# A split matmul on one core: twenty Strassen pairs in place of eighteen, evacuations shared out per visit, and one transfer per pair of row blocks

## The chip, the core and the metric

The kernel runs on one core of a Trainium2 chip. The metric is the device time of the whole program in microseconds, the median of several runs. The engines named below are TensorE (PE, with its weight loads PEld), VectorE (DVE), ScalarE (ACT), GpSimd (POOL) and SyncE (SP).

## What is computed

```python
batch, m, k, n = 16, 512, 1024, 768
grad_weight = np.einsum('bmk,bmn->kn', input, grad_output)     # float32
```

With the batch folded into the rows this is one product: the transpose of X (8192 x 1024) times G (8192 x 768), summed over 8192 rows. The result is 1024 x 768 in float32.

## The kernel before, in words

**Slices and pairs.** The 8192 rows are 64 slices of 128 rows; a slice is the depth of one matmul. Slices come in 32 pairs (u = 0 to 31), each with a tile xp (128 partitions x 2 x 1024, bfloat16) and gp (128 x 2 x 768). GpSimd issues the transfers (lines 99 to 102), one for each slice's part of gp and of xp, and they convert float32 to bfloat16 on the way. Only slice 0 and the x part of slice 1 come as float32 through SyncE and ScalarE (lines 72 to 77) and are cast by VectorE and ScalarE (`round_by`, line 191). The pool holds 14 pairs (`PAIRS_HELD`).

**Products.** The result is cut in four: A (upper half of the rows, left half of the columns), B (upper right), C (lower left) and D (lower right), each 512 x 384. A slice alone ("s" in `LOADS`) adds one product to each of A, B, C and D: 4 products. A pair treated as a 2 x 2 block ("P") takes Strassen's way with 7 products in place of 8: two of them go straight into A and D, and five into the side sums m, n, o, p and q (`macc`). Each product is 4 matmuls of 128 x 384, one for each of 4 PSUM banks (q = 0 to 3), so that a slice costs 16 matmuls, and a pair 28 in place of 32. `LOADS` says which pairs are taken in which way: 18 are "P".

**Sums.** A "P" pair needs sums of its operands before its products, six VectorE instructions (lines 114 to 143): g1 (`ge` 0 and 1), g2 (`ge` 2), g3 (in place in `gp`), x1 (`xe` 0 and 1), x2 (`xe` 2) and x3 (in place in `xp`). What a product needs of them: m needs x2 and g2; n and q need x1; o and p need g3; A and D need x3 and g1 (`operands`, line 212).

**Shares.** Near the end the five side sums are added to and taken from the result, 24 VectorE instructions: `top1` to `top3` for the upper half, `low1` to `low3` for the lower half, each for 4 values of q. Eight of them (`top3`, `low3`) are 384 wide, the others 768.

**Visits, banks and the order.** PSUM has eight banks, in two slots of four. A visit in `ORDER` continues one product stream in an open slot: "A17" multiplies all items of stream A up to but not including its 17th (counted over all items for A, B, C and D; the streams m to q count pairs alone). With "!" it then closes: each bank is evacuated into SBUF (`acc` or `macc`). Before, the banks 0 and 1 are evacuated by VectorE, which adds the bank to the sum (line 284; below such an instruction is called V), and the banks 2 and 3 by ScalarE, which copies (line 280). So that ScalarE need only copy, the sum so far is copied into the bank when the visit opens (line 256), and the matmuls go on adding to it. A visit of one item does its four matmuls and then evacuates; a visit of several finishes bank after bank.

**What sets the order.** PE, VectorE and ScalarE run in exactly the order in which the program issues (`manual_schedule`, line 70). `ORDER` is written out: the figure ahead of the letter says how many of the waiting sums and shares (the list `filler`) VectorE does before the visit; the four figures behind "!" say how many it does before each bank's evacuation. An instruction of VectorE that waits holds all behind it. GpSimd's transfers are ordered by the tile framework, which has eight of them in flight.

**The tail.** The last visit, D46 before, does its last bank in two parts of 256 and 128 columns (line 312). Finished parts of A, B, C and D are stored by SyncE (lines 288 and 325).

A step from `ORDER`, as an example: `3m10!1,0,0,0` is three sums, then stream m up to pair 10, one sum, and the evacuation of its four banks.

Of the kernel before, what the change touches and what calls it, by code (L numbers as in the profile page):

```python
# [7 lines left out]

P = 128

LOADS = "sssPssssPsPsPPPPPPPPPPPPPPPsssss"


ORDER = (
    "A1 C1!0,0,0,0 D1 D2!0,0,0,0 A2 B1 B2 B3!0,0,0,0 A3 C4!0,0,0,0 A4 A5 B4 B5 B6!0,0,0,0 A6 "
    "C6!0,0,0,0 D6 6A7 D8!0,0,0,0 A8 o1!0,0,0,0 A9 B8!0,0,0,0 A10 C9 C10!0,0,0,0 A11 "
    "q1!0,0,0,0 A12 D12 A13 D13 A14!0,0,0,0 D14!0,0,0,0 n1 C14!0,0,0,0 B13 B14 6n2!0,0,0,0 "
    "B15 p1 p2!0,0,0,0 B16!0,0,0,0 m1 m2 A17!0,0,1,1 D18 4m3!0,0,0,0 D19 D20 B18!0,0,0,0 "
    "C18!0,0,1,1 A21 D21 4A22!0,0,0,0 D22 o4!2,0,1,1 q4 2D23!3,0,0,0 q5 n5 3n6!0,0,0,0 q6 p5 "
    "p6!6,0,0,0 q7 o7!1,0,0,2 m7 3q8!1,0,0,0 m8 A25 A26!5,0,0,0 m9 p9!1,0,0,2 D27 "  # L20
    "3m10!1,0,0,0 D28 n10!3,0,0,2 D29 A29!2,0,1,1 o11 2o12!2,0,0,0 D30 q12 4D31!1,0,0,0 q13 "
    "p12 p13!5,0,0,0 q14 m14!2,1,0,1 n14!2,0,0,2 q15 o15 4q16!0,0,0,0 o16 D34!2,0,1,1 "
    "A34!1,1,0,3 o17 n17 3o18!0,0,0,0 n18!0,0,0,0 A35 m18!0,0,0,0 A39 q18!0,0,0,0 p18!0,0,0,0 "
    "A41 A43 C22 C24 C26 A46!13,0,0,0 B23 B24 B28!6,0,0,0 C28!5,0,0,0 D46!0,0,0,0 "
).split()

WARMUP = [512] * 10 + [128] * 2
PAIRS_HELD = 14
SUMS_HELD = 9

CARRIED = (2, 3)
COPIED = CARRIED or (1, 3)


@with_exitstack
def kernel(
# [6 lines left out]
    nc = tc.nc  # L43
# [4 lines left out]
    _, _, N = grad_output.shape  # L48
    S = B * M // P
    KH = K // 2  # L50
    NH = N // 2
    Q = KH // P

    X = input.rearrange("b m k -> (b m) k")
    G = grad_output.rearrange("b m n -> (b m) n")
# [17 lines left out]
    gf = pairs.tile([P, N], f32, name="gf", tag="gp")  # L73
# [18 lines left out]
    xg = []  # L92
    for u, kind in enumerate(LOADS):
        pool = pairs if u else head
        xp = pool.tile([P, 2, K], bf16, name="xp", tag="xp")
        gp = pool.tile([P, 2, N], bf16, name="gp", tag="gp")
        for h in range(2):
            s = 2 * u + h
            if s > 0:
                nc.gpsimd.dma_start(out=gp[:, h, :], in_=G[s * P : (s + 1) * P, :])  # L100
            if s > 1:
                nc.gpsimd.dma_start(out=xp[:, h, :], in_=X[s * P : (s + 1) * P, :])  # L102
            if kind == "s":
                items.append(("s", xp[:, h, :], gp[:, h, :]))
        if kind == "P":
            items.append(("P", xp, gp))
        xg.append((xp, gp))
# [68 lines left out]
    filler = []  # L176
    for i, item in enumerate(items):
        if item[0] == "P":
            filler += [(f, i) for f in (sum_g1, sum_g2, sum_g3, sum_x1, sum_x2, sum_x3)]
    if filler:  # L180
        filler += [(f, q) for q in range(Q) for f in (top1, top2, top3)]
        filler += [(f, q) for q in range(Q) for f in (low1, low2, low3)]
    filler.reverse()

    def fill(n):
        for _ in range(n):
            f, i = filler.pop()
            f(i)


    def round_by(engine, dst, src, c0, c1):
        copy = nc.vector.tensor_copy if engine == "DVE" else nc.scalar.copy
        copy(out=dst[:, c0:c1], in_=src[:, c0:c1])  # L193

    x0, x1, g0 = items[0][1], items[1][1], items[0][2]
# [34 lines left out]
    def sum_of(p, q):  # L230
        if p in SLOT:
            return macc[:, SLOT[p], q, :]
        row = q if p in "AB" else Q + q
        return acc[:, row, 0:NH] if p in "AC" else acc[:, row, NH:N]

    done = {p: 0 for p in streams}
    fresh = {p: True for p in streams}
    slots = [0, 1]
    used = set()

    def visit(p, upto, close, ahead, last):
        items_now = streams[p][done[p] : upto]
        done[p] = upto
        opening = p not in opened
        if opening:

            tail = p in "ABCD" and streams[p][upto - len(items_now)] > LAST_PAIR - 2
            slot = slots.pop(0)
            banks = []
            for q in range(Q):  # L250
                name = f"bank{slot * Q + q}"
                bank = psum.tile([P, 512], f32, name=name)[:, 0:NH]
                carried = q in CARRIED and not fresh[p] and not tail
                if carried:
                    assert name in used
                    nc.scalar.copy(out=bank, in_=sum_of(p, q))  # L256
                used.add(name)
                banks.append((bank, carried))
            opened[p] = (slot, banks)
        slot, banks = opened[p]  # L260
        final = upto == len(streams[p])

        def mm(q, j):
            stat, mov = operands(p, items_now[j], q)
            bank, carried = banks[q]
            nc.tensor.matmul(  # L266
                bank,
                stat,
                mov,
                start=opening and j == 0 and not carried,  # L270
                stop=close and j == len(items_now) - 1,
                skip_group_check=carried,
            )

        def shut(q):
            fill(ahead[q])
            bank, carried = banks[q]
            dst = sum_of(p, q)
            if carried or (fresh[p] and q in COPIED):
                nc.scalar.copy(out=dst, in_=bank)  # L280
            elif fresh[p]:
                nc.vector.tensor_copy(out=dst, in_=bank)  # L282
            else:
                nc.vector.tensor_add(out=dst, in0=bank, in1=dst)  # L284
            if final and p in "ABCD":
                row = q if p in "AB" else Q + q
                c0 = 0 if p in "AC" else NH
                nc.sync.dma_start(out=OUT[:, row, c0 : c0 + NH], in_=dst)

        if len(items_now) == 1:  # L290
            for q in range(Q):
                mm(q, 0)
            if close:
                for q in range(Q):
                    shut(q)
        else:
            for q in range(Q):
                if last and q == Q - 1 and opening:
                    break
                for j in range(len(items_now)):  # L300
                    mm(q, j)
                if close:
                    shut(q)
            else:
                q = None
            if q is not None:

                fill(ahead[q])
                dst = sum_of(p, q)
                row = q if p in "AB" else Q + q  # L310
                b0 = 0 if p in "AC" else NH
                for c0, c1, name in ((0, 256, None), (256, NH, f"bank{slots[0] * Q}")):
                    bank = banks[q][0] if name is None else psum.tile([P, 512], f32, name=name)
                    for j in range(len(items_now)):
                        stat, mov = operands(p, items_now[j], q)
                        nc.tensor.matmul(  # L316
                            bank[:, 0 : c1 - c0],
                            stat,
                            mov[:, c0:c1],
                            start=j == 0,  # L320
                            stop=j == len(items_now) - 1,
                        )
                    d = dst[:, c0:c1]
                    nc.vector.tensor_add(out=d, in0=bank[:, 0 : c1 - c0], in1=d)  # L324
                    nc.sync.dma_start(out=OUT[:, row, b0 + c0 : b0 + c1], in_=d)
        if close:
            fresh[p] = False
            del opened[p]
            slots.append(slot)

    for n, step in enumerate(ORDER):
        step, _, ahead = step.partition("!")
        at = next(c for c in step if c.isalpha())
        before, upto = step.split(at)
        if n == 2:
            round_by("DVE", g0, gf, NH, N)
            round_by("DVE", x1, xf[1], 4 * P, 6 * P)
            round_by("ACT", x1, xf[1], 6 * P, 8 * P)
            round_by("DVE", x1, xf[1], 0, 2 * P)
            round_by("ACT", x1, xf[1], 2 * P, 4 * P)  # L340
        fill(int(before or 0))
        ahead = [int(a) for a in ahead.split(",")] if ahead else None
        visit(at, int(upto), ahead is not None, ahead, n == len(ORDER) - 1)
    assert not filler and not opened


# [28 lines left out]
```

## Time and profile before

| | |
|---|---|
| time, median of 3 | 169.47 us (169.4 to 169.53) |
| span of the profile | 168.0 us |
| granted TensorE clock | 1.000 |
| PE, DVE, ACT, POOL busy | 161.3, 124.1, 73.3, 66.6 us |
| one matmul of 128 x 384, by the records | 327 ns (it overlaps the next) |
| V: evacuating add of a bank, 128 x 384 | 553 ns |
| ScalarE copy out of a bank, into a bank | 483 ns, 496 ns |
| a share of 768, of 384 columns | 954 ns, 558 ns |
| x and g transfers of GpSimd | 62 and 63, 8.5 us from issue to landing |
| DMA, GB/s written in the middle | 206 to 211 |

How to read it: the records of matmuls overlap, so their duration is not their spacing. An instruction of VectorE or ScalarE can also start before the one ahead of it has ended, which is why spacings are read from the starts in the timeline. A wait of an engine that isn't the bottleneck costs nothing. A slot, below, is the time of one matmul, and slots are counted from the first matmul that is not a warm-up: the matmul numbers follow from `ORDER`.

### The profile page before, as it was taken

The page shows a single profiled execution, that of the slowest core. Times are in us where ns is not written, and L with a number is a line of the kernel's source. Part 1 is how long each engine was busy: PE and PEld are TensorE (multiplying, and loading weights), DVE is VectorE, ACT ScalarE, POOL GpSimd, SP SyncE. Part 2 cuts the span into 40 slices and gives each one's busy share as a digit, 9 for nine tenths or more (in the row PEclk, how much of TensorE's full clock was granted, in tenths as well). Part 3 has the DMA queues.
Part 4 walks back from the last instruction along what each step waited for, and adds up shares of the span by engine and source line. Part 5 has one row for each costly group of instructions (what it writes and reads, how often), then busy time and mean ns, then how long its engine had stood idle before and what let it go on. Part 6 is the DMA issues. An engine that isn't in the chain of part 4 may idle for free.

```text
span 168.0 us, 2737 instructions
## 1 busy us (share of the span) xinstructions
PE 161.3 (96%) x976; PEld 95.3 (57%) x976; DVE 124.1 (74%) x248; ACT 73.3 (44%) x172; POOL 66.6 (40%) x129
## 2 busy tenths in 40 slices
PE   8799989999999999999999899999999999989991
PEld 2365545656666566555566466655666666556561
DVE  0642755307667686999999988999996179999992
ACT  3536608435456473654554643365655451000000
POOL 7444444454355444455444554445526430000000
PEclk9999999999999999999999999999999999999999
DMA  5999999999999999999999999999999999331546
GB/s 180 287 209 209 206 210 209 208 206 211 209 208 209 208 209 208 209 207 208 209 208 209 207 207 209 211 207 208 208 208 210 208 208 208 65 134 53 187 151 223
DMA packets 21036, 33.39 MB, mean 199 GB/s; under 512 B 2336, under 2 KB 12832, under 8 KB 21024
## 3 DMA queue, kind: packets, MB, share of 16 engines
q0 software_dynamic: 18000, 28.65, 93.2%
q1 hardware_dynamic: 2736, 3.54, 6.0%
q10 hardware_dynamic: 288, 1.05, 1.6%
q8 instruction: 7, 0.11, 0.3%
q14 instruction: 5, 0.04, 0.1%
HBM read 58.72 MB, written 3.15 MB: 368 GB/s over the span
## 4 chain that ended last, share of the span: by engine, by line
PE 74%; DMA 12%; DVE 9%; POOL 2%; issue 1%; DVEq 0%; POOLq 0%
PE bank L266 73%; DMA xp<-in_input_dram 12%; DVE acc L152 5%; DVE acc L163 1%; POOL gp L100 1%; DVE macc L284 1%; PE bank L316 1%; POOL xp L102 1%; DVE xp L143 0%; DVE xe L134 0%; DVE acc L284 0%; DVE gp L129 0%; DVE acc L324 0%; DVE ge L124 0%; DVE xe L138 0%
## 5 line engine op out<-in xcount | busy, mean ns | idle before, releaser
L266 PE MATMUL bank<-gp,xp 128*128 128x384 bf16 x582 | 102.2, 327 | 1.9 <-DVE gp L193 0.9
L266 PEld LDWEIGHTS <-xp 128*128 128x128 bf16 x724 | 70.6, 98 | 51.1 <-issue 2.7
L102 POOL DMA_DIRECT2D xp<-in_input_dram x62 | 33.0, 532 | 42.9 <-DMA xp<-in_input_dram 30.4
L100 POOL DMA_DIRECT2D gp<-in_grad_output_dram x63 | 33.7, 536 | 27.5 <-DMA gp<-in_grad_output_dram 16.0
L284 DVE TENSOR_TENSOR acc<-bank,acc 128x384 f32<-128x384 f32 x53 | 27.0, 553 | 15.2 <-PE bank L266 15.0
L280 ACT COPY acc<-bank 128x384 f32<-128x384 f32 x46 | 20.5, 483 | 31.6 <-PE bank L266 31.6
L280 ACT COPY macc<-bank 128x384 f32<-128x384 f32 x46 | 20.5, 483 | 31.0 <-PE bank L266 31.0
L266 PE MATMUL bank<-ge,xp 128*128 128x384 bf16 x142 | 28.7, 326 | 0.7 <-DVE xp L143 0.6
L266 PEld LDWEIGHTS <-xe 128*128 128x128 bf16 x216 | 21.1, 98 | 14.3 <-issue 0.4
L266 PE MATMUL bank<-gp,xe 128*128 128x384 bf16 x144 | 26.3, 326 | 0.0
L284 DVE TENSOR_TENSOR macc<-bank,macc 128x384 f32<-128x384 f32 x36 | 18.6, 554 | 7.7 <-PE bank L266 7.6
L256 ACT COPY bank<-acc 128x384 f32<-128x384 f32 x38 | 17.2, 495 | 0.0
L256 ACT COPY bank<-macc 128x384 f32<-128x384 f32 x36 | 16.3, 496 | 0.0
L152 DVE TENSOR_TENSOR acc<-acc,macc 128x768 f32<-128x768 f32 x16 | 15.3, 954 | 0.3
L266 PE MATMUL bank<-ge,xe 128*128 128x384 bf16 x72 | 13.0, 326 | 0.0
L143 DVE TENSOR_TENSOR xp<-xp 128x1024 bf16<-128x1024 bf16 x18 | 12.4, 688 | 0.0
L134 DVE TENSOR_TENSOR xe<-xp 128x1024 bf16<-128x1024 bf16 x18 | 12.4, 687 | 0.0
L120 DVE TENSOR_TENSOR ge<-gp 128x768 bf16<-128x768 bf16 x18 | 10.0, 553 | 1.0 <-DMA gp<-in_grad_output_dram 0.8
L129 DVE TENSOR_TENSOR gp<-gp 128x768 bf16<-128x768 bf16 x18 | 9.9, 553 | 0.0
L282 DVE COPY acc<-bank 128x384 f32<-128x384 f32 x8 | 4.1, 553 | 7.7 <-PE bank L266 7.7
L282 DVE COPY macc<-bank 128x384 f32<-128x384 f32 x10 | 5.1, 553 | 3.8 <-PE bank L266 3.8
L138 DVE TENSOR_TENSOR xe<-xp 128x512 bf16<-128x512 bf16 x18 | 7.6, 421 | 0.0
(18 smaller groups left out, 27.5 us busy)
## 6 DMA issues: line engine op xcount, KB each, us to landing
xp<-in_input_dram POOLq DMA_DIRECT2D x62, 256.0 KB, 8.5
gp<-in_grad_output_dram POOLq DMA_DIRECT2D x63, 192.0 KB, 8.5
out_dram<-acc SPq DMA_DIRECT2D x15, 192.0 KB, 2.0
xf<-in_input_dram ACTq DMA_DIRECT2D x2, 512.0 KB, 5.0
gf<-in_grad_output_dram SPq DMA_DIRECT2D x2, 192.0 KB, 4.5
out_dram<-acc SPq DMA_DIRECT2D x1, 128.0 KB, 2.1
out_dram<-acc SPq DMA_DIRECT2D x1, 64.0 KB, 1.8
```

What stands on the lines that cost most here:

```text
L100: nc.gpsimd.dma_start(out=gp[:, h, :], in_=G[s * P : (s + 1) * P, :])
L102: nc.gpsimd.dma_start(out=xp[:, h, :], in_=X[s * P : (s + 1) * P, :])
L120: nc.vector.tensor_add(out=ge[:, 0:2, :], in0=g[:, :, 0, :], in1=g[:, :, 1, :])
L129: nc.vector.tensor_sub(out=g[:, 1:3, :], in0=g[:, 1:3, :], in1=g[:, 3::-3, :])
L134: nc.vector.tensor_add(out=xe[:, 0:2, :].rearrange("p a k -> p (a k)"), in0=xp[:, 0, :], in1=xp[:, 1, :])
L143: nc.vector.tensor_sub(out=x[:, 1:3, :], in0=x[:, 1:3, :], in1=x[:, 0::3, :])
L152: nc.vector.tensor_add(out=dst, in0=dst, in1=macc[:, slots, q, :])
L256: nc.scalar.copy(out=bank, in_=sum_of(p, q))
L266: nc.tensor.matmul(bank, stat, mov, start=opening and j == 0 and not carried, stop=close and j == len(items_now) - 1, skip_group_check=car ...
L280: nc.scalar.copy(out=dst, in_=bank)
L282: nc.vector.tensor_copy(out=dst, in_=bank)
L284: nc.vector.tensor_add(out=dst, in0=bank, in1=dst)
```

## The change

Twenty pairs are taken by Strassen's way in place of eighteen: eight pairs as slices first (16 slices), then twenty "P", then four pairs as slices. Each visit has its own number of banks for ScalarE, written after a colon (":4" all four, ":0" none, no figure where the stream is open or VectorE takes all); the constants `CARRIED` and `COPIED` go. The shares have an order of their own (`SHARES`), and some of them stand earlier. From pair 8 on (slice 16), one transfer brings the whole g tile of a pair and one the whole x tile, with rows 2p and 2p + 1 of the pair on partition p: a partition then reads one run of 6144 or 8192 bytes of float32 where it read two of 3072 or 4096. The order of rows within a pair does not matter, as all are summed. The cast of the right half of G's slice 0 moves ahead of the second visit. It is all meant to do fewer matmuls while VectorE's work still fits.

```diff
@@ -8,28 +8,35 @@
 
 P = 128
 
-LOADS = "sssPssssPsPsPPPPPPPPPPPPPPPsssss"
+LOADS = "ssssssssPPPPPPPPPPPPPPPPPPPPssss" 
 
 ORDER = (
-    "A1 C1!0,0,0,0 D1 D2!0,0,0,0 A2 B1 B2 B3!0,0,0,0 A3 C4!0,0,0,0 A4 A5 B4 B5 B6!0,0,0,0 A6 "
-    "C6!0,0,0,0 D6 6A7 D8!0,0,0,0 A8 o1!0,0,0,0 A9 B8!0,0,0,0 A10 C9 C10!0,0,0,0 A11 "
-    "q1!0,0,0,0 A12 D12 A13 D13 A14!0,0,0,0 D14!0,0,0,0 n1 C14!0,0,0,0 B13 B14 6n2!0,0,0,0 "
-    "B15 p1 p2!0,0,0,0 B16!0,0,0,0 m1 m2 A17!0,0,1,1 D18 4m3!0,0,0,0 D19 D20 B18!0,0,0,0 "
-    "C18!0,0,1,1 A21 D21 4A22!0,0,0,0 D22 o4!2,0,1,1 q4 2D23!3,0,0,0 q5 n5 3n6!0,0,0,0 q6 p5 "
-    "p6!6,0,0,0 q7 o7!1,0,0,2 m7 3q8!1,0,0,0 m8 A25 A26!5,0,0,0 m9 p9!1,0,0,2 D27 "
-    "3m10!1,0,0,0 D28 n10!3,0,0,2 D29 A29!2,0,1,1 o11 2o12!2,0,0,0 D30 q12 4D31!1,0,0,0 q13 "
-    "p12 p13!5,0,0,0 q14 m14!2,1,0,1 n14!2,0,0,2 q15 o15 4q16!0,0,0,0 o16 D34!2,0,1,1 "
-    "A34!1,1,0,3 o17 n17 3o18!0,0,0,0 n18!0,0,0,0 A35 m18!0,0,0,0 A39 q18!0,0,0,0 p18!0,0,0,0 "
-    "A41 A43 C22 C24 C26 A46!13,0,0,0 B23 B24 B28!6,0,0,0 C28!5,0,0,0 D46!0,0,0,0 "
+    "A1:4 C1:4!0,0,0,0 B2:4!0,0,0,0 A2 D1:2 A3!0,0,0,0 D2 D3 D4 C4:4!0,0,0,0 D5 B5:2 D6!0,0,0,0 "
+    "B6 A6:2 B7 B8 A7 A8 A9!0,0,0,0 B9 C9:2 C10!0,0,0,0 B11 D11:2 B12 D13!0,0,0,0 A14:2 A15 B14 "
+    "B16!0,0,0,1 C16:2!2,0,1,2 A16 A17 D17:4!3,0,1,2 A18!0,0,0,0 n2:4!0,0,1,0 o1:2 m2:4 o2 "
+    "2o3!3,0,0,0 m3!0,0,0,0 q3:4!1,2,0,0 p1:4 p2 p4 3D20:3!3,0,0,1 p5 q5:2!2,0,0,0 A21:2!1,0,0,2 "
+    "p6 o6:2!2,0,0,1 n6:2 3p7!2,1,0,0 n7 m7:2!2,1,0,1 n8 q8:2!2,0,0,1 D24:2!2,0,1,1 n9 "
+    "o9:2!2,0,0,1 A25:2 2n10!2,0,0,0 A26 m10:2!2,0,0,1 p11:2 3A27!3,0,0,0 p12 D27:2!1,0,0,2 "
+    "q12:2!1,0,1,1 p13 o13:3!3,0,2,1 p14 n13:2!1,0,0,1 m14:2!1,0,1,2 p15 D30:2!2,0,0,1 "
+    "A31:2!1,1,0,2 q16:2!1,1,0,1 p16 n16:2!2,1,0,0 p17 1m17:2!2,0,0,1 o17:2!2,0,0,2 D34:2!1,0,1,1 "
+    "p18 p19 A34:4!4,1,1,0 p20!0,0,0,0 D35:0 o20:2!2,0,0,1 q20:2!1,0,0,1 n20:2!0,1,0,1 "
+    "D37!0,0,0,0 m20:4!0,0,1,0 A35:0 A36 B19:0 B20 A39 A41 A44!11,0,0,0 B23 C17:0 B24!2,0,0,0 "
+    "C24!2,0,0,0 D44:0!4,0,0,0 "
+).split()
+
+
+SHARES = (
+    "l20 l21 t20 t21 t22 t23 t30 t31 t32 t33 t10 t11 t12 t13 l22 l23 l10 l11 l12 l13 l30 l31 l32 "
+    "l33 "
 ).split()
 
 WARMUP = [512] * 10 + [128] * 2
 PAIRS_HELD = 14
 SUMS_HELD = 9
 
-CARRIED = (2, 3)
-COPIED = CARRIED or (1, 3)
+MERGED = 8
 
 
 @with_exitstack
@@ -94,11 +101,15 @@
         pool = pairs if u else head
         xp = pool.tile([P, 2, K], bf16, name="xp", tag="xp")
         gp = pool.tile([P, 2, N], bf16, name="gp", tag="gp")
+        if u >= MERGED:
+            rows = slice(2 * u * P, 2 * (u + 1) * P)
+            nc.gpsimd.dma_start(out=gp, in_=G[rows, :].rearrange("(p m) n -> p m n", m=2))
+            nc.gpsimd.dma_start(out=xp, in_=X[rows, :].rearrange("(p m) k -> p m k", m=2))
         for h in range(2):
             s = 2 * u + h
-            if s > 0:
+            if s > 0 and u < MERGED:
                 nc.gpsimd.dma_start(out=gp[:, h, :], in_=G[s * P : (s + 1) * P, :])
-            if s > 1:
+            if s > 1 and u < MERGED:
                 nc.gpsimd.dma_start(out=xp[:, h, :], in_=X[s * P : (s + 1) * P, :])
             if kind == "s":
                 items.append(("s", xp[:, h, :], gp[:, h, :]))
@@ -177,9 +188,8 @@
     for i, item in enumerate(items):
         if item[0] == "P":
             filler += [(f, i) for f in (sum_g1, sum_g2, sum_g3, sum_x1, sum_x2, sum_x3)]
-    if filler:
-        filler += [(f, q) for q in range(Q) for f in (top1, top2, top3)]
-        filler += [(f, q) for q in range(Q) for f in (low1, low2, low3)]
+    share_by = {"t1": top1, "t2": top2, "t3": top3, "l1": low1, "l2": low2, "l3": low3}
+    filler += [(share_by[c[:2]], int(c[2:])) for c in SHARES]
     filler.reverse()
 
     def fill(n):
@@ -238,7 +248,7 @@
     slots = [0, 1]
     used = set()
 
-    def visit(p, upto, close, ahead, last):
+    def visit(p, upto, byact, close, ahead, last):
         items_now = streams[p][done[p] : upto]
         done[p] = upto
         opening = p not in opened
@@ -250,19 +260,21 @@
             for q in range(Q):
                 name = f"bank{slot * Q + q}"
                 bank = psum.tile([P, 512], f32, name=name)[:, 0:NH]
-                carried = q in CARRIED and not fresh[p] and not tail
+                act = q >= Q - byact
+                carried = act and not fresh[p]
+                assert not (carried and tail)
                 if carried:
                     assert name in used
                     nc.scalar.copy(out=bank, in_=sum_of(p, q))
                 used.add(name)
-                banks.append((bank, carried))
+                banks.append((bank, carried, act))
             opened[p] = (slot, banks)
         slot, banks = opened[p]
         final = upto == len(streams[p])
 
         def mm(q, j):
             stat, mov = operands(p, items_now[j], q)
-            bank, carried = banks[q]
+            bank, carried, _ = banks[q]
             nc.tensor.matmul(
                 bank,
                 stat,
@@ -274,9 +286,9 @@
 
         def shut(q):
             fill(ahead[q])
-            bank, carried = banks[q]
+            bank, _, act = banks[q]
             dst = sum_of(p, q)
-            if carried or (fresh[p] and q in COPIED):
+            if act:
                 nc.scalar.copy(out=dst, in_=bank)
             elif fresh[p]:
                 nc.vector.tensor_copy(out=dst, in_=bank)
@@ -330,17 +342,19 @@
 
     for n, step in enumerate(ORDER):
         step, _, ahead = step.partition("!")
+        step, _, byact = step.partition(":")
         at = next(c for c in step if c.isalpha())
         before, upto = step.split(at)
+        if n == 1:
+            round_by("DVE", g0, gf, NH, N)
         if n == 2:
-            round_by("DVE", g0, gf, NH, N)
             round_by("DVE", x1, xf[1], 4 * P, 6 * P)
             round_by("ACT", x1, xf[1], 6 * P, 8 * P)
             round_by("DVE", x1, xf[1], 0, 2 * P)
             round_by("ACT", x1, xf[1], 2 * P, 4 * P)
         fill(int(before or 0))
         ahead = [int(a) for a in ahead.split(",")] if ahead else None
-        visit(at, int(upto), ahead is not None, ahead, n == len(ORDER) - 1)
+        visit(at, int(upto), int(byact or 0), ahead is not None, ahead, n == len(ORDER) - 1)
     assert not filler and not opened
```

## The prediction

> **What bounds it now.** I read the page's busy table first, then its slices, then the waits of PE, then the timeline at the longest wait.
>
> ```profile
> PE 161.3 (96%) x976; PEld 95.3 (57%) x976; DVE 124.1 (74%) x248; ACT 73.3 (44%) x172; POOL 66.6 (40%) x129
> ...
> PE   8799989999999999999999899999999999989991
> ...
> DMA  5999999999999999999999999999999999331546
> ```
>
> TensorE is busy in every slice, and the DMA engines are full up to slice 34 (143 us). So both are close to a bound, and the chain of waits (PE 74%, DMA 12%) agrees. The waits of PE and of its weight loads are few:
>
> ```profile
> PE bank L266 <- DVE gp L193: 0.9, 1, 0.9
> ...
> PE bank L266 <- DVE xp L143: 0.6, 1, 0.6
> PE bank L266 <- DVE acc L284: 0.6, 1, 0.6
> PE bank L266 <- DMA xp<-in_input_dram: 0.4, 1, 0.4
> ```
>
> One wait each; a listed wait starts at the end of the last matmul, which lies 0.165 us behind the next free slot (duration 327 ns, spacing 162.5), so the slots lost are 0.165 longer: 0.74 us for D29 waiting on sum x3, 0.73 for B23 waiting on a bank of A46. Here is the first, from VectorE's and PE's timelines:
>
> ```profile
> 94.11 1.02 DVE L284 TENSOR_TENSOR macc<-bank,macc 128x384 f32<-128x384 f32 x2
> 95.04 0.42 DVE L138 TENSOR_TENSOR xe<-xp 128x512 bf16<-128x512 bf16 x1
> 95.37 0.69 DVE L143 TENSOR_TENSOR xp<-xp 128x1024 bf16<-128x1024 bf16 x1
> 95.97 0.56 DVE L120 TENSOR_TENSOR ge<-gp 128x768 bf16<-128x768 bf16 x1
> ...
> 96.12 0.34 PE L266 MATMUL bank<-ge,xp 128*128 128x384 bf16 x1 [0.58 <-DVE xp L143]
> ```
>
> From such starts I take spacings, since durations overlap: an evacuating add "V" 0.47 us, g1 0.46, g2 0.27, g3 0.47, x1 0.60, x2 0.33, x3 0.60 (2.73 a pair), 0.15 from the end of a sum's spacing to the matmul that uses it (95.97 to 96.12), 0.20 from the last slot of a bank to its V. ScalarE: 0.38 a copy out, 0.42 a copy into a bank.
>
> **What the Trainium skill says.** "TensorE: Matmul & The Clock Gate", Back-to-back issue gap: N/2.4 + 2.5 ns, for 384 columns 162.5 ns; the trace agrees (48 matmuls from 148.86 to 156.65 us, 162.3 each). "VectorE: DVE Perf Modes", The perf-mode tier table: tensor_tensor runs at twice the rate on bf16 in SBUF and at the single rate with a PSUM operand; the trace agrees (768 bf16 elements and 384 fp32 from a bank both 553 ns). "DMA: Bandwidth & Descriptors", Why small descriptors are slow: each packet carries a fixed overhead; Measured: at best 425 GB/s for large transfers. The trace writes 208 GB/s of bf16, so reads 416 of fp32: at most 2% is left for larger packets.
>
> **The change, part by part.**
> *Two more pairs.* 18 pairs and 28 slices alone are 18x28 + 28x16 = 952 matmuls; 20 and 24 are 944. Gain 8 x 0.1625 = 1.30 us, on the path.
> *VectorE and ScalarE.* Counted through both orders: VectorE has 12 sums more (+5.5 us) and 20 evacuations fewer (-9.4); ScalarE 24 copies out and 10 into banks more (+13.3, to 87). Both stay below PE. Their totals cost nothing; what counts is which instruction stands ahead of the one that PE needs.
> *Head.* Before, the cast of G's right half waits behind two evacuations (7.61) and PE starts its 9th matmul at 8.01; sum x3 of the first pair then costs 0.3 (22.5 to 22.76) and slice 8 about 0.6, so matmul 101 starts at 24.18 and 112 at 25.97. After, C1 and B2 leave VectorE free: G's right half lands at 1.17 + 5.2 = 6.4, is cast by 6.8. But ScalarE's casts of slice 1 (landed 7.1) now stand behind C1's four copies (6.67 + 4x0.38), done 8.97: matmul 13 starts at 9.02, 16 at 9.5. Then 96 x 0.1625 = 15.6, slice 2 (lands 10.85) 0.1, slice 8 (24.1) 0.15, two banks at 0.1: matmul 112 at 25.55. Gain 0.4. With slices alone first, PE takes 2.6 us a slice against 2.2 of DMA, so no later slice is waited for.
> *VectorE's order in the pair phase.* D29's 0.74 goes. New places are found in the same way: from the V ahead, add spacings, and compare with the slots between. p6 needs g3, which stands behind A21's second V: 0.20 + 0.47 + 0.27 + 0.47 + 0.15 = 1.56 us, but from that bank's last slot to p6 there are 6 slots (0.98): loss 0.58. n8 needs x1 behind V g3 V: 2.36 + the rest of its queue against 12 slots (1.95): 0.40. p13: 1.56 against 8 slots: 0.26. p15 needs g3 behind V g1 g2: 2.02 against 8 slots: 0.72. q16: about 0.18; n9 0.12; D34 0.05. p14 has none left once p13 has moved it. Sum 2.3. By the same method D29 before comes out at 0.75, where the trace has 0.74.
> *Banks.* Where a visit of one item closes and its banks are opened 4 slots later, bank 0 is late by 0.20 + 0.55 - 0.65 = 0.1. Some eight such places explain the 0.5 us of the middle of before that the two waits do not; after has some four: 0.25. m7's copies into banks (four copies out ahead of them) cost 0.3, but inside n8's 0.40.
> *Merged transfers.* 125 issues become 77, with the same bytes. A pair lands 4.40 us after the last (GpSimd issues an x transfer each 2.20 us, and the page has 8.5 us from issue to landing); with 2% it would be 4.31. Bounds: 4.31 and 4.40, I take 4.40. xp of pair u lands at 8.5 + 4.4u: u = 9 at 48.1, its x3 is done at 49.8, A18 needs it at 50.3. gp of u = 24 is issued after xp of 25: lands at 116.8, g3 done 118.2, p17 needs it at 7.35 + 672 x 0.1625 + 2.3 = 118.85 (7.35 is 25.55 less 112 slots). So nothing is gained or lost as long as PE is not earlier than this. Buffers are no limit: at least 256 slots (41 us) lie between the release of a pair's buffer and the need of its next content, and eight transfers in flight are now 17.6 us.
> *Tail.* Some shares move ahead of A44. From D37's first V (slot 798) to A44's last: 8 V, 6 long shares at 0.88, 4 short at 0.47, 1.76 for l22, l23: 12.7 us or 78 slots, so slot 876; C17 opens those banks at 880. B23's 0.73 goes. But D44 holds 7 items a bank in place of 12: its five stores are issued within 2 us (0.4 each on SyncE) and follow C24's four. Before, they are 2 us apart. Bounds 0.1 and 0.9 (five stores one after another at SyncE and half of one's 2.0 us); I take 0.45.
>
> Sum: before ends its last slot at 164.48 = 25.97 + 840 x 0.1625 + 0.74 + 0.73 + 0.54. After: 25.55 + 832 x 0.1625 + 2.3 + 0.25 = 163.3. Less 1.15, plus 0.45: -0.7, so 168.8 us.
>
> **Rivals.**
> *PE runs through.* If evacuations are really quicker to follow than I think, the 2.3 go: then gp of u = 24 binds at 118.2 against 116.5 and about 1.7 is lost there, unless merging gives the 2% (gp at 115.4, loss 0.3). Between 166.8 and 168.2; 167.4. For it: the page shows just one such wait in before. Against: it lies where the method puts it.
> *VectorE's queue costs more.* Another 0.15 at each of some ten tight places (six more have under 0.4 us of slack), and stores at the upper bound: 1.5 + 0.4 more, 170.4, slower than before. For it: there are nine places with no slack, and before has one. Against: each loss also moves PE later for the next.
> *Merged transfers are slower.* 5% (4.62 a pair) would land gp of 24 at 120.5 and cost 3 us: 171.8. Against: larger packets carry less overhead.
> *A draw.* The tail at its upper bound and a little more in the queue: 169.4.
>
> **Numbers.** The forecast 0.43, PE runs through 0.20, draw 0.17, VectorE's queue 0.14, slower transfers 0.06. Faster by over 0.2% (below 169.13): 0.43 x 0.9 + 0.20 = 0.59. Same (to 169.81): 0.20. Slower 0.21. The range from 167.2 to 170.4 leaves out the slow transfers and the ends of the others.
>
> **What would show it.** About 944 + 16 matmul records; PE waits on DVE gp (g3) near 66.5, 99 and 107 us and on xe near 76 and 114, 2.3 in sum; no wait for D29's kind of 0.6 nor at A44; casts of slice 1 on ScalarE near 8.9; pairs landing 4.3 to 4.4 us apart; stores that close up at the end. The forecast is wrong if these waits are absent, or if PE waits for the DMA in the pair phase.

## The result, and the profile after

The changed kernel takes 168.14 us (median of 4 runs, 168.07 to 168.65) against 169.5 us for the kernel before on the same chip. The ratio is 0.9926, with a 95% interval from 0.9905 to 0.9947: 0.74% or some 1.25 us faster. The profiled span goes from 168.0 to 166.3 us.

From the page of the changed kernel, the busy table and two of the rows of 40 slices:

```profile
PE 159.8 (96%) x963; PEld 93.5 (56%) x963; DVE 118.6 (71%) x240; ACT 87.6 (53%) x206; POOL 41.1 (25%) x81
...
PE   8799999999999999999999999899999999999992
...
DMA  5999999999999999999999999999999999105555
```

TensorE is still the bound. Work went from VectorE to ScalarE as counted (240 instructions for 248, 206 for 172), and GpSimd issues 48 transfers fewer. 963 records for 976 are the 8 matmuls of the two more pairs, and 5 of the tail, whose split bank has 7 items in place of 12. The waits of PE (columns: total, times, longest, in us):

```profile
PE bank L278 <- DVE xp L203: 0.8, 2, 0.6
...
PE bank L278 <- DVE gp L140: 0.7, 2, 0.6
...
PE bank L278 <- DVE xe L145: 0.2, 1, 0.2
...
PE bank L278 <- DMA xp<-in_input_dram: 0.2, 1, 0.2
```

D29's wait on x3 and B23's on a bank are gone. In their place stand waits on `gp L140`, which is g3, and `xe L145`, which is x1, at the places that the prediction named. PE's timeline has three of them (start, duration; the wait in brackets is 0.165 shorter than the lost slots):

```profile
66.49 2.76 PE L278 MATMUL bank<-gp,xp 128*128 128x384 bf16 x16 [0.15 <-DVE gp L140]
...
75.98 2.77 PE L278 MATMUL bank<-gp,xe 128*128 128x384 bf16 x16 [0.23 <-DVE xe L145]
...
107.82 0.81 PE L278 MATMUL bank<-gp,xp 128*128 128x384 bf16 x4 [0.55 <-DVE gp L140]
```

From the starts of all matmuls (start to start, less 0.1625) the slots lost in the middle are these:

| place | predicted | lost, us |
|---|---|---|
| A21's third bank, 65.20, then p6, 66.49 | 0.58 | 0.25 + 0.32 |
| n8, 75.98 | 0.40 | 0.40 |
| n9, 81.38 | 0.12 | 0.18 |
| p13, 98.60, and p14, 101.91 | 0.26 and 0 | 0.31 + 0.06 |
| p15, 107.82 | 0.72 | 0.72 |
| q16, 113.68 | 0.18 | 0.18 |
| D34, 124.36 | 0.05 | 0.27 |
| other openings of banks | 0.25 | 0 |
| sum | 2.56 | 2.69 |

A21's third bank waits for ScalarE's copy of the sum into it, which starts only at 64.65, behind two copies out:

```profile
64.65 0.91 ACT L268 COPY bank<-acc 128x384 f32<-128x384 f32 x2
```

The reckoning of PE's whole stretch closes with these: slot 112 starts at 24.96, plus 832 x 0.1625, plus 2.69 is 162.85, where the last matmul starts at 162.84. In the kernel before it starts at 164.43. The end is thus 1.6 earlier (1.15 predicted): the eight slots fewer are 1.30, slot 112 starts 1.0 earlier (24.96 for 25.97), and after slot 112 0.7 more is lost than before (2.7 for 2.0). The rest of the span follows it: from the last matmul's end to the end of the span it is 3.38 us before and 3.24 after, where 0.45 more was predicted. Before, in the timeline of the last 10 us:

```profile
160.67 3.34 DVE L284 TENSOR_TENSOR acc<-bank,acc 128x384 f32<-128x384 f32 x7
...
161.25 3.31 SPq L288 DMA_DIRECT2D out_dram<-acc  x7
...
164.65 0.90 SPq L325 DMA_DIRECT2D out_dram<-acc  x2
```

And after:

```profile
160.88 1.62 DVE L296 TENSOR_TENSOR acc<-bank,acc 128x384 f32<-128x384 f32 x3
...
163.16 0.82 SPq L337 DMA_DIRECT2D out_dram<-acc  x2
```

Before, VectorE was behind with its shares and made the last seven sums of whole banks in one go, so nine stores stood one behind another at SyncE from 161.25 on, 0.46 to 0.50 us apart. That is the closing up that the prediction expected of the changed kernel; the kernel before had more of it.

### The profile page after: what moved, and what is told of

Same layout as the page of the kernel before. It is cut to its first block, busy times and chain, and to the rows that moved or that the text cites. A ratio compares the mean times of both kernels' runs of the same rounds, so it can differ in the third digit from the quotient of the medians.

```text
span 166.3 us, 2688 instructions
## 1 busy us (share of the span) xinstructions
PE 159.8 (96%) x963; PEld 93.5 (56%) x963; DVE 118.6 (71%) x240; ACT 87.6 (53%) x206; POOL 41.1 (25%) x81
## 3 DMA queue, kind: packets, MB, share of 16 engines
q10 hardware_dynamic: 288, 1.05, 1.7%
## 4 chain that ended last, share of the span: by engine, by line
PE 76%; DVE 16%; DMA 5%; POOL 1%; issue 1%; DVEq 0%; POOLq 0%
PE bank L278 75%; DVE macc L296 5%; DMA xp<-in_input_dram 5%; DVE gp L140 2%; DVE xe L145 2%; DVE acc L296 2%; DVE ge L131 2%; DVE xp L154 1%; POOL gp L111 1%; DVE ge L135 1%; DVE xe L149 1%; PE bank L328 0%; DVE acc L336 0%; DVEq L296 0%; POOLq L373 0%
## 5 line engine op out<-in xcount | busy, mean ns | idle before, releaser
L278 PEld LDWEIGHTS <-xp 128*128 128x128 bf16 x697 | 67.6, 98 | 49.4 <-issue 1.9
L278 PE MATMUL bank<-gp,xp 128*128 128x384 bf16 x537 | 92.4, 326 | 2.0 <-DVE xp L203 0.8
L292 ACT COPY acc<-bank 128x384 f32<-128x384 f32 x55 | 24.4, 487 | 31.2 <-PE bank L278 31.1
L296 DVE TENSOR_TENSOR acc<-bank,acc 128x384 f32<-128x384 f32 x46 | 23.7, 552 | 21.3 <-PE bank L278 21.0
L292 ACT COPY macc<-bank 128x384 f32<-128x384 f32 x61 | 27.3, 492 | 20.2 <-PE bank L278 20.1
L278 PEld LDWEIGHTS <-xe 128*128 128x128 bf16 x240 | 23.2, 98 | 16.6 <-DVE xe L145 1.4
L107 POOL DMA_DIRECT2D xp<-in_input_dram x24 | 12.7, 530 | 36.9 <-DMA xp<-in_input_dram 20.3
L106 POOL DMA_DIRECT2D gp<-in_grad_output_dram x24 | 12.7, 530 | 32.7 <-PE bank L278 19.5
L268 ACT COPY bank<-macc 128x384 f32<-128x384 f32 x43 | 19.3, 490 | 0.0
L145 DVE TENSOR_TENSOR xe<-xp 128x1024 bf16<-128x1024 bf16 x20 | 13.7, 684 | 0.7 <-DMA xp<-in_input_dram 0.7
L140 DVE TENSOR_TENSOR gp<-gp 128x768 bf16<-128x768 bf16 x20 | 11.0, 551 | 0.0
L113 POOL DMA_DIRECT2D xp<-in_input_dram x14 | 7.5, 538 | 9.0 <-DMA xp<-in_input_dram 6.4
L111 POOL DMA_DIRECT2D gp<-in_grad_output_dram x15 | 8.2, 547 | 6.1 <-DMA gp<-in_grad_output_dram 4.6
L294 DVE COPY acc<-bank 128x384 f32<-128x384 f32 x2 | 1.0, 554 | 10.6 <-PE bank L278 10.6
```

The costliest lines, as they stand in the source:

```text
L106: nc.gpsimd.dma_start(out=gp, in_=G[rows, :].rearrange("(p m) n -> p m n", m=2))
L107: nc.gpsimd.dma_start(out=xp, in_=X[rows, :].rearrange("(p m) k -> p m k", m=2))
L140: nc.vector.tensor_sub(out=g[:, 1:3, :], in0=g[:, 1:3, :], in1=g[:, 3::-3, :])
L145: nc.vector.tensor_add(out=xe[:, 0:2, :].rearrange("p a k -> p (a k)"), in0=xp[:, 0, :], in1=xp[:, 1, :])
L278: nc.tensor.matmul(bank, stat, mov, start=opening and j == 0 and not carried, stop=close and j == len(items_now) - 1, skip_group_check=car ...
```

## Experiments

All ratios are to the kernel before, measured beside it on the same chip; a ratio is followed by its 95% interval. A difference between two kernels below is the difference of their ratios times 169.7 us. The runs come from three chips (e1 to e4, e5 to e8, e9 and e10), so that e5_all_order against e2_all, e7_all_single_order against e4_all_single and e10_a21 against e5_all_order compare across chips; the changed kernel was measured in a set of its own. The theory to start with: what the changed kernel still loses is VectorE's order (2.4 us), the transfers' size is worth nothing, and the moved evacuations bring what they bring by taking V out from between the sums. The two more pairs, the order of the shares and the earlier cast were not tried one by one; for them there is the count of slots above.

**One wait taken away (e1_p15).** The sums g1, g2 and g3 that p15 needs are done ahead of m14's first V, not after its two.

```diff
-m14:2!1,0,1,2
+m14:2!4,0,0,0
```

> One place alone: the sums g1, g2 and g3 of pair 14 are done before both evacuating adds of m14 (m14!4,0,0,0 for 1,0,1,2), nothing else is changed. Theory (each wait of PE on VectorE's order is paid in full): the wait of p15, 0.72 us at 107.8 us in the changed kernel, goes, and the time falls by 0.6 to 0.75 us to about 167.4 us. Rival (another engine or the DMA is right behind, so that removing one wait only moves it): less than 0.25 us is gained, and a new wait of PE shows after 108 us.

167.9 us, 0.9895 (0.9881 to 0.9908): 0.5 us better than the changed kernel, where 0.6 to 0.75 was expected; the two intervals overlap a little, so the trace has to decide. VectorE's timeline of the changed kernel, in which g3 (L140) ends the queue V, V, g1, g2, g3:

```profile
105.35 1.21 DVE L296 TENSOR_TENSOR macc<-bank,macc 128x384 f32<-128x384 f32 x2
106.48 0.55 DVE L131 TENSOR_TENSOR ge<-gp 128x768 bf16<-128x768 bf16 x1
...
107.21 0.55 DVE L140 TENSOR_TENSOR gp<-gp 128x768 bf16<-128x768 bf16 x1
```

And of e1_p15, where the two V come last and nobody waits for them:

```profile
106.28 0.55 DVE L140 TENSOR_TENSOR gp<-gp 128x768 bf16<-128x768 bf16 x1
106.75 1.02 DVE L296 TENSOR_TENSOR macc<-bank,macc 128x384 f32<-128x384 f32 x2
```

p15's 0.72 is gone from the starts, the other places keep their values to 0.01, and PE's last matmul starts 0.31 earlier. The other 0.41 of this profile is at its head: its first six matmuls start 0.3 us apart, those of the changed kernel's profile mostly 0.1625, and slot 112 is 0.42 later.

**All of them (e2_all).** The same for p6, n8, n9, p13, q16 and D34.

```diff
-A21:2!1,0,0,2
+A21:2!3,0,0,0
-m7:2!2,1,0,1
+m7:2!4,0,0,0
-D24:2!2,0,1,1
+D24:2!3,0,0,1
-q12:2!1,0,1,1
+q12:2!3,0,0,0
-o13:3!3,0,2,1
+o13:3!6,0,0,0
-m14:2!1,0,1,2
+m14:2!4,0,0,0
-A31:2!1,1,0,2
+A31:2!4,0,0,0
-o17:2!2,0,0,2
+o17:2!4,0,0,0
```

> All places where PE waited on a sum (p6, n8, n9, p13 with p14, p15, q16, D34) get their sums ahead of the evacuating adds. Theory: 2.4 us of waits go, but p17 then comes at 116.0 us, while the g tile of pair 24 lands at 115.2 and its three sums take 1.4 more, so 0.65 us is paid there to the DMA: gain 1.8 us, about 166.3 us. Rival (VectorE's load as a whole is the limit, so delayed evacuations make PE wait for banks in their place): gain under 0.7 us, and waits of PE on evacuating adds.

167.36 us, 0.9862 (0.9849 to 0.9876): 1.1 us better than the changed kernel, not 1.8. The waits that were aimed at are gone, but others have come. From its waits:

```profile
DVE ge L131 <- DMA gp<-in_grad_output_dram: 1.5, 1, 1.5
...
PE bank L278 <- DVE xe L149: 0.7, 1, 0.7
...
PE bank L278 <- DVE macc L296: 0.3, 1, 0.3
```

The first line is the cause: with PE and VectorE earlier, VectorE stands for 1.5 us before g1 of pair 24, whose G lands at 115.29, and its queue is late for x2 of m17 (0.90 lost at 118.53) and for a bank (0.50 at 123.27). The waits at VectorE's order had been hiding the transfers. In the two profiles, some 2.0 us of losses go and 1.3 come. At D34 the moved sums gain nothing in any case: its wait on x3 becomes a wait on the bank that the delayed V frees, of which 0.29 is left even in e5_all_order and e10_a21 below.

**The transfers alone (e3_single, e4_all_single).** The changed kernel and e2_all, each with one transfer per slice as before.

```diff
-MERGED = 8
+MERGED = 32
```

> The changed kernel with one transfer per slice for all pairs, as before the change, all else kept. Theory: transfers of pairs land 4.40 us apart in place of 4.31, the g tile of pair 24 at about 116.7 in place of 115.2 us, and p17 needs its sums at 118.4: so 0 to 0.4 us is lost, time 168.1 to 168.5 us. Rival (the merged transfers brought the gain): over 1 us is lost, and PE waits for the DMA or for sums that waited for it all through the pair phase.

> The sums moved ahead at all places, and one transfer per slice. Theory: with the waits gone p17 comes at 116.0 us, but its sums are done at 118.1, so the DMA takes back about 2.1 of 2.4 us: 0.3 us better than with single transfers alone, and 1.5 us worse than the merged one with the same order. Rival (single transfers are as good): the same as the merged kernel with this order within 0.3 us.

e3_single: 169.41 us, 0.998 (0.997 to 0.999), 0.9 us worse than the changed kernel. e4_all_single: 169.39 us, 0.9985 (0.9972 to 0.9998), no better than e3_single although the sums are moved (0.3 better was expected, which the intervals don't exclude), and 2.1 us behind e2_all, where 1.5 was expected. The 0.9 us lies between the theory (0 to 0.4) and the rival (over 1). So the merged transfers are worth 0.9 us of the change's 1.25, as GpSimd's order stands, and the prediction's "nothing is gained or lost" falls. VectorE's timeline in e3_single, at g1 of pair 24 and at m17's x2:

```profile
117.03 0.56 DVE L131 TENSOR_TENSOR ge<-gp 128x768 bf16<-128x768 bf16 x1 [1.11 <-DMA gp<-in_grad_output_dram]
...
119.78 0.42 DVE L149 TENSOR_TENSOR xe<-xp 128x512 bf16<-128x512 bf16 x1
```

And PE's:

```profile
120.25 1.80 PE L278 MATMUL bank<-ge,xe 128*128 128x384 bf16 x10 [0.47 <-DVE xe L149]
```

VectorE gets pair 24's G at 117.0, where the prediction said 116.8, and p17 finds its g3 in time, as predicted too. But g1 holds everything behind it in VectorE's queue: g2, g3, a V, x1, another V, and then x2, which m17 needs: 117.03 plus 0.47, 0.27, 0.47, 0.47, 0.60 and 0.47 is the 119.78 of the line. m17 loses 0.64 and D34 0.48 (0.27 in the changed kernel); a third loss is 0.15 at A17, 46.62.

**The order of the transfers (e5_all_order, e6_order, e7_all_single_order).** In GpSimd's timeline the x transfers of pairs 24 and 25 (L107) go out before G of pair 24 (L106), although the program has G first. This is e2_all:

```profile
91.80 0.53 POOL L107 DMA_DIRECT2D xp<-in_input_dram  x1 [1.89 <-DVE ge L135]
93.65 0.53 POOL L107 DMA_DIRECT2D xp<-in_input_dram  x1 [1.32 <-DVE acc L296]
96.11 0.53 POOL L107 DMA_DIRECT2D xp<-in_input_dram  x1 [1.93 <-PE bank L278]
97.96 0.53 POOL L106 DMA_DIRECT2D gp<-in_grad_output_dram  x1 [1.32 <-PE bank L278]
```

With GpSimd in the program's order as well, G of pair 24 goes out at 93.7 and not 98.0. e5_all_order is e2_all with this edit, e6_order the changed kernel with it, e7_all_single_order is e4_all_single with it.

```diff
-    ctx.enter_context(tc.manual_schedule(engines={E.PE, E.DVE, E.Activation}))
+    ctx.enter_context(tc.manual_schedule(engines={E.PE, E.DVE, E.Activation, E.Pool}))
```

> The sums moved ahead at all places, and GpSimd's transfers issued in the order of the pairs (g tile, x tile, g tile, x tile) to the end, where they otherwise stand x x x g g g g from pair 23 on. Theory (the late g tiles are what limits the version with all sums moved): the g tile of pair 24 lands at about 110.5 in place of 115.3 us, VectorE no longer waits for it, PE's waits at 116.7, 118.5 and 123.3 us (0.14, 0.90, 0.50) go, and slice 2 lands earlier at the head (up to 0.4): 1.4 to 1.9 us better than that version, about 165.7 us. Rival (the DMA's rate, not its order, is the limit, as the queue is full to 143 us): the same within 0.4 us, with the waits moved to x tiles.

> The changed kernel with nothing but the order of GpSimd's transfers put right. Theory: PE's waits on sums are set by VectorE's order there and not by data, so only the head gains: 0.1 to 0.4 us better than the changed kernel, the waits of p6, n8, p13 and p15 stay as they are. Rival (data is what sums wait for): over 0.8 us better.

> Sums moved ahead, transfers in the order of the pairs, but one transfer per slice. Theory (the order, not the size of the transfers, made single transfers lose): 0.2 to 0.7 us slower than the merged version with the same order, from sums that wait for tiles which land up to 2 us later. Rival (the rate of single transfers is too low in itself): 1.5 us slower or more.

e5_all_order: 166.38 us, 0.9802 (0.9788 to 0.9815), 1.0 us better than e2_all. Its GpSimd, at the same time:

```profile
91.86 0.53 POOL L107 DMA_DIRECT2D xp<-in_input_dram  x1 [1.91 <-PE bank L278]
93.72 0.53 POOL L106 DMA_DIRECT2D gp<-in_grad_output_dram  x1 [1.33 <-DVE acc L296]
96.15 0.53 POOL L107 DMA_DIRECT2D xp<-in_input_dram  x1 [1.91 <-DVE xp L154]
```

G of pair 24 lands at 110.5 in place of 115.3, and the losses at 118.5 and 123.3 are gone (0.29 is left at 122.45). That is less than expected; what is missing is a new loss at the head: a wait of 0.57 for the X of slice 7 at 22.35 (0.73 lost), which is treated at the end. e6_order, 168.32 us, 0.9917 (0.9903 to 0.993), is the changed kernel within the interval (0.1 to 0.4 better was expected): p6 to q16 keep their losses to 0.01, and the head wins 0.36 at slice 2 and loses 0.75 at 22.25. e7_all_single_order, 167.0 us, 0.9837 (0.9823 to 0.985), is 0.6 us behind e5_all_order, as expected: in the right order, the transfers' size is worth 0.35%, and the order is worth 2.5 us to single transfers (0.9985 to 0.9837).

**Two banks at each visit (e8_two).** The choice of ScalarE's banks undone: every ":3" and ":4" in the order becomes ":2".

```diff
-A1:4 C1:4!0,0,0,0 B2:4!0,0,0,0
+A1:2 C1:2!0,0,0,0 B2:2!0,0,0,0
...
-D17:4!3,0,1,2
+D17:2!3,0,1,2
...
-o13:3!3,0,2,1
+o13:2!3,0,2,1
```

> The changed kernel with two banks for ScalarE at every visit that had three or four (as before the change), two for VectorE. Theory: 24 or so more evacuating adds stand ahead of sums in VectorE's queue; A18 and p6 then wait about 1.0 and 0.7 us more, p14 and p20 0.6 each: 1.3 to 2.2 us slower than the changed kernel, about 169.8 us. Rival (VectorE has idle time enough, 71% busy): the same within 0.3 us.

172.25 us, 1.0143 (1.013 to 1.0157): 3.7 us slower than the changed kernel, well above what was expected. VectorE has 24 instructions more and is 129.4 us busy, still 41 less than the span of 170.4. From its waits:

```profile
PE bank L278 <- DVE gp L140: 2.1, 4, 0.6
PE bank L278 <- DVE xp L154: 0.9, 1, 0.9
...
PE bank L278 <- DVE xe L145: 0.6, 1, 0.6
```

From the starts, against the changed kernel: A18 on x3 loses 1.05 where it lost nothing, p20 0.67 where it lost nothing, p14 0.71 for 0.06, n8 0.79 for 0.40, p6 0.65 for 0.32, q5 0.22 for nothing; p15, q16 and D34 lose what they lost. That is 3.3 us more after slot 112; the rest is at the head. The expectation named A18, p6, p14 and p20, 2.9 us in all, and took 1.3 to 2.2 of it, as if a loss at one place spared the next. These four lose 2.7 more, and n8 and q5 come on top: they add up instead. My reading, argued and not tested alone: V waits for PE's banks, so that VectorE moves later together with PE, and the time by which it is late for the next sum stays.

**Merged transfers in the kernel before (e9_before_merged).** The kernel before, with the four lines for `u >= MERGED` alone.

```diff
+MERGED = 8
...
+        if u >= MERGED:
+            rows = slice(2 * u * P, 2 * (u + 1) * P)
+            nc.gpsimd.dma_start(out=gp, in_=G[rows, :].rearrange("(p m) n -> p m n", m=2))
+            nc.gpsimd.dma_start(out=xp, in_=X[rows, :].rearrange("(p m) k -> p m k", m=2))
...
-            if s > 0:
+            if s > 0 and u < MERGED:
...
-            if s > 1:
+            if s > 1 and u < MERGED:
```

> The kernel before, with one thing added: from slice 16 on one transfer of G and one of X for two slices (two neighbouring rows per partition). Theory: the transfers' size is worth time only where PE is early enough to meet the landings. In the kernel before PE waits for no G of a pair (its two waits on data in the pair phase and after are on VectorE's x3 and on a bank), and it is later than the changed kernel by some 1.5 us; so the time stays within 0.3 us of before (ratio 0.998 to 1.002). Rival: larger transfers bring by themselves the 0.9 us that they were worth in the changed kernel (ratio 0.995). A second rival: the later first landing of a pair's rows (both slices only at once) makes PE wait where slices alone follow each other: slower by 0.3 us or more.

171.0 us, 1.0073 (1.006 to 1.0087): 1.2 us slower, the second rival. PE's timeline:

```profile
46.16 0.81 PE L271 MATMUL bank<-gp,xe 128*128 128x384 bf16 x4
48.10 2.77 PE L271 MATMUL bank<-gp,xp 128*128 128x384 bf16 x16 [1.13 <-DMA xp<-in_input_dram]
```

1.29 us of slots are lost here and nowhere else that before does not lose: in the order of before, pair 9 is taken as two slices, and its first slice is needed at once. Alone, slice 18's X lands at 46.00; as half of a pair it lands at 48.06. Some 0.4 of the loss may come from a transfer of instructions at 43.55 us (the last section): G of pair 9 lands 2.55 us after the X ahead of it, where the G before and the G after take 1.86 and 1.85. D29's 0.75 and B23's 0.73 are unchanged, and larger packets bring nothing, as PE waits for no later landing. So the merging and the new `LOADS`, with no slice taken alone between the first merged pair and the last "P", belong together: merging alone costs 0.7%, and the rest of the change without merging (e3_single) brings 0.2%, where both bring 0.74%.

**One bank more for VectorE (e10_a21).** e5_all_order with A21's third bank left to VectorE.

```diff
-A21:2!3,0,0,0
+A21:1!3,0,0,0
```

> The fastest kernel so far (all sums of a visit ahead of its first evacuation, transfers in the program's order), and A21 gives ScalarE one bank instead of two. Theory: the 0.25 us at 65.8 us is A21's third bank waiting for ScalarE's copy of its sum into it; with one bank the copies are one fewer and it goes, while VectorE's fourth evacuation there (0.47 us) hides ahead of p6, whose sums are already done: 0.2 us less than that kernel (ratio 0.9788 against its 0.9802). Rival: the copy of the last bank waits in its place, or VectorE's queue passes the 0.47 on to p6 or n6: no gain, or 0.2 slower.

166.09 us, 0.9786 (0.9773 to 0.9799), the fastest of all. Against e5_all_order it is 0.27 us; the intervals overlap, but the lost 0.25 at 65.84 is gone from the starts and nothing has taken its place. The longest waits left to its matmuls:

```profile
PE bank L278 <- DMA xp<-in_input_dram: 0.6, 1, 0.6
PE bank L278 <- DVE xp L203: 0.5, 1, 0.5
PE bank L278 <- ACT xp L203: 0.2, 1, 0.2
```

All three are in the first 23 us. From there to the end it loses 0.4 us (0.11 at q16, 0.29 at D34).

## Why the prediction was right or wrong

**Direction and size.** Faster was right, and the time is 0.66 us (0.4%) below the forecast, inside its range. In the profiled executions the miss is 1.0 us (1.7 shorter where 0.7 was forecast): 0.59 is the tail, 0.44 PE's end. It is larger there because the profiled execution of before took 169.8 us, 0.3 above its median. The time alone would also fit the upper end of the rival "PE runs through" (166.8 to 168.2), but the trace decides: PE does not run through, the waits on VectorE's order are there (2.4 us). Nor did the other rivals come: the waits are not larger by 0.15 at each place; the transfers are not slower.

**The 1.30 for eight matmuls: right.** 832 slots of 0.1625 us close the reckoning above. "Back-to-back issue gap" in "TensorE: Matmul & The Clock Gate" of the Trainium skill, which the prediction quotes for it, gives this formula for a matmul by itself, and a shorter gap for a stream of long ones. The stream measured here keeps to the formula (162.3 ns at 384 columns), and the measurement decides.

**The 2.3 us of new waits: right.** Seven places were named and all seven lose, six of them by the predicted amount to 0.06. D34 was undersized (0.05, measured 0.27), and p14 keeps 0.06 where none was left. p6's 0.58 was the right total: 0.25 of it falls on A21's third bank ahead, and what delays A21 comes off p6's wait. That bank is also the only opening which loses anything, and it waits for a copy of ScalarE and not for a V, as the term of 0.25 for openings had it. So this term comes to nothing, D34 and three smaller excesses (n9, p13, p14) stand in its place, and that the sum is right to 0.13 is in part luck. e1_p15 and e2_all show the mechanism: with the sums ahead of the V, the waits on VectorE's sums go.

**The tail's 0.45: wrong.** The step that failed is "Before, they are 2 us apart". They were nine stores in a row at 0.46 to 0.50 us, as the timeline of before shows. The changed kernel wins 0.1 in the tail where 0.45 was to be lost.

**The head's 0.4: right in kind.** Slot 112 starts at 24.96, not 25.55. Of this, 0.5 is there by slot 16: ScalarE's copies of C1 begin at 6.20 and not at 6.67, since this profile's first eight matmuls are mostly 0.1625 apart; 0.35 are waits for slice 8 and banks that are absent; slice 2 costs 0.36 and not 0.1. In e1_p15, whose first matmuls are 0.3 apart, slot 112 is at 25.38. How often each head comes in the timed runs was not seen, since only one execution of each kernel is profiled.

**"Nothing is gained or lost" by merging: wrong.** Pairs land 4.3 us apart, as the lower bound said. What failed is "p17 needs it at 118.85": the first use of the landed tile was checked, and not the instructions of other pairs' work that stand behind g1 in VectorE's queue. Of them x2 for m17 is the tight one. Merging is worth 0.9 us in the changed kernel. The sum came out near all the same, and by luck: the predicted sum had no loss there, and with the merged transfers there is none.

**VectorE's and ScalarE's totals "cost nothing": right, with a limit.** e8_two has VectorE at 76% and is 2.2% slower. The total is no bound, but 24 evacuations of 0.47 us ahead of sums that PE needs are worth 3.7 us.

## What to carry to other kernels

Where engines run in a written order, work out for each operand the instructions that stand ahead of it on the producing engine, back to the last one that waits; do this for every instruction queued behind a landing, not just for its first user. When 2.0 us of such waits were removed here (e2_all), waits at the next limit took 1.3 of it back: so check the transfers' issue order (GpSimd's, here left to the framework) before tuning an order further. Larger transfers pay only where all that they bring is needed together; where half of it is needed first, they cost the landing of the other half: here it came 2 us later, and 1.3 us of it was paid.

## What the runs showed of the hardware

**A transfer of instructions every 21 us.** Once in about 21 us a transfer of 16 KB for instructions runs through one of the DMA engines. From the DMA answer for e5_all_order between 19.7 and 22.8 us (share of 16 engines):

```profile
q0 software_dynamic: 393, 0.63, 110.9%
q8 instruction: 1, 0.02, 1.9%
```

1.9% of 16 engines for 3.1 us is 0.94 us on one engine. The x transfer then in flight (slice 7) lands at 22.30, 2.6 us after the transfer ahead of it, where at this size 1.2 to 1.3 us is the rule, and its neighbour follows at 22.76. GpSimd's next issue waits with it:

```profile
19.95 0.53 POOL L111 DMA_DIRECT2D gp<-in_grad_output_dram  x1 [0.42 <-DMA gp<-in_grad_output_dram]
22.58 0.53 POOL L113 DMA_DIRECT2D xp<-in_input_dram  x1 [2.10 <-DMA xp<-in_input_dram]
```

At the head, where PE takes slices as they land, this costs e5_all_order, e6_order and e10_a21 0.72 to 0.75 us, and it takes back what an earlier start had won. Later transfers of this kind cost PE nothing in these three kernels that the starts show. In the kernel before it falls on the X of slice 8, which lands at 24.13, and is most likely the 0.6 lost there. That the one causes the other is read from their falling together in these profiles; moving the transfer was not tried.

**First matmuls at half rate.** In some profiles the first matmuls after the warm-up start 0.3 us apart: five spacings in e1_p15, three in before, two in e9_before_merged. In those of the changed kernel, e2_all and e10_a21 all are near 0.1625. The page's clock row is the same in each. The warm-up's instructions are the same in all of them; what decides it was not found.

**Packets.** Runs of 6 and 8 KB read per partition instead of 3 and 4 moved 210 to 217 GB/s (mean 213) in most slices of the page, where single transfers moved 206 to 211 (mean 208). That is some 2%, as much as the prediction had left from the 425 GB/s of "DMA: Bandwidth & Descriptors" in the Trainium skill (Measured): 213 written as bfloat16 are 426 read as float32. Single slices lie above it (217, so 434 read), so it is no hard bound. The runs got longer and the transfers half as many at once, and no run separates the two.
